# Matmul with rotary embedding: tiles worked in pairs over three PSUM banks, one multiply per pair, and one tile in four transposed by VectorE

## The chip, the cores and the metric

One core of a Trainium2 chip. The time is the device time of one execution in microseconds. The kernel before ran at 168.18 us, the median of three runs (166.9 to 168.86). A "beat" below is the time TensorE takes for one tile, or one pair of tiles, in the steady part of the kernel. All verdicts and ratios use runs of the state called fast; the medians are over all runs, and those of e1, e5 and e10 include runs of the slow state.

## The reference

```python
# x (16, 512, 768), weight (768, 768), cos and sin (512, 64), 12 heads of 64 columns, all fp32
y = np.matmul(x, weight).reshape(batch, seq, n_heads, head_dim)
y1, y2 = y[..., :32], y[..., 32:]
out1 = y1 * cos1 - y2 * sin1
out2 = y2 * cos2 + y1 * sin2
out = np.concatenate([out1, out2], axis=-1).reshape(batch, seq, hidden)
```

There are 16 x 512 = 8192 rows, which is 64 tiles of 128 rows. For every tile the contraction runs over the 768 columns of x, and the kernel before turns every tile (columns onto partitions) for the matmuls: 384 transposes on TensorE, six a tile, in its profile.

## The kernel before

Every tile is loaded by the SyncE ring (a ring is the queue of transfers that one engine's sequencer issues), cast to fp16 by ScalarE, turned by six TensorE transposes into PSUM (the memory that TensorE writes its results to), copied back by ScalarE, multiplied with the weights by twelve matmuls, and then combined by two VectorE multiplies and one GpSimd (POOL) add. The ScalarE ring stores.

```python
def load(i):
    xss[i] = xpool.tile([P, H], FP32, tag="xs", name="xs")
    nc.sync.dma_start(out=xss[i], in_=xv[i // SB, i % SB])
...
def transpose(i, eng):
    xc = x16.pop(i)
    pt = pt_pool.tile([P, NKT, P], FP16, tag="pt", name="pt")
    for kt in range(NKT):
        nc.tensor.transpose(pt[:, kt, :], xc[:, ts(kt, P)], ident)
    xTT[i] = tpool.tile([P, NKT, P], FP16, tag="xT", name="xT")
    copy(eng, xTT[i], pt)
...
for i in range(FIRST, NMB):
    if i + AHEAD - FIRST < NMB:
        load(i + AHEAD - FIRST)
    if i + 1 < NMB:
        transpose(i + 1, nc.scalar)
    if 4 < i + 2 < NMB:
        cast(i + 2, nc.scalar)
    if i < NMB - 1:
        for kt in range(NKT):
            mm(i, kt)
        rope_whole(i)
        store(i - 3)
```

Of the kernel before, what the change touches and what calls it, by code (L numbers as in the profile page):

```python
# [10 lines left out]
FP32 = mybir.dt.float32  # L11
# [6 lines left out]
def kernel(  # L18
# [16 lines left out]
    NKT = H // P  # L35
    NMB = B * S // P
    SB = S // P
    NSPLIT = [(0, 512), (512, H - 512)]
    HALVES = [(0, H // 2), (H // 2, H // 2)]
    FIRST = 3  # L40
    AHEAD = 8


    xv = x.rearrange("b (p r) h -> b r p h", r=SB)
    ov_dram = out.rearrange("b (p r) h -> b r p h", r=SB)
# [3 lines left out]
    cos_sb = konst.tile([P, SB, D], FP32)  # L49
    tee_sb = konst.tile([P, SB, D], FP32)  # L50
    w_raw = konst.tile([P, NKT, H], FP32)
    w_sb = konst.tile([P, NKT, H], FP16)

    xpool = ctx.enter_context(tc.tile_pool(name="xpool", bufs=AHEAD + 3))
    cpool = ctx.enter_context(tc.tile_pool(name="cpool", bufs=4))
    tpool = ctx.enter_context(tc.tile_pool(name="tpool", bufs=FIRST + 2))
    rpool = ctx.enter_context(tc.tile_pool(name="rpool", bufs=4))
    opool = ctx.enter_context(tc.tile_pool(name="opool", bufs=5))
    pt_pool = ctx.enter_context(tc.tile_pool(name="pt", bufs=2, space=bass.MemoryType.PSUM))
    py_pool = ctx.enter_context(tc.tile_pool(name="py", bufs=3, space=bass.MemoryType.PSUM))  # L60

    cold = konst.tile([P, 512], FP16)
    cold_ps = pt_pool.tile([P, 512], FP32, tag="pt", name="cold_ps")

    xss, x16, xTT, psys, ovs = {}, {}, {}, {}, {}
# [7 lines left out]
    def load(i):  # L73
        xss[i] = xpool.tile([P, H], FP32, tag="xs", name="xs")
        nc.sync.dma_start(out=xss[i], in_=xv[i // SB, i % SB])  # L75

    wv = weight.rearrange("(kt p) n -> p kt n", p=P)

    def load_w(kt):
        nc.sync.dma_start(out=w_raw[:, kt], in_=wv[:, kt])  # L80

    def cast_w(kt):
        nc.vector.tensor_copy(out=w_sb[:, kt], in_=w_raw[:, kt])  # L83

    def cast(i, eng):
        x16[i] = cpool.tile([P, H], FP16, tag="xc", name="xc")
        copy(eng, x16[i], xss.pop(i))

    def transpose(i, eng):
        xc = x16.pop(i)  # L90
        pt = pt_pool.tile([P, NKT, P], FP16, tag="pt", name="pt")
        for kt in range(NKT):
            nc.tensor.transpose(pt[:, kt, :], xc[:, ts(kt, P)], ident)  # L93
        xTT[i] = tpool.tile([P, NKT, P], FP16, tag="xT", name="xT")
        copy(eng, xTT[i], pt)

    def mm(i, kt, parts=NSPLIT):
        if i not in psys:
            psys[i] = py_pool.tile([P, 2, 512], FP32, tag="psy", name="psy").rearrange(
                "p b n -> p (b n)"  # L100
            )
        for noff, nsz in parts:
            nc.tensor.matmul(  # L103
                psys[i][:, ds(noff, nsz)],
                xTT[i][:, kt, :],
                w_sb[:, kt, ds(noff % H, nsz)],
                start=(kt == 0),
                stop=(kt == NKT - 1),
            )

    def rope(i, c0, n, ps, add_eng):
        sb = i % SB
        nh = n // D
        tv = rpool.tile([P, H], FP32, tag="tv", name="tv")[:, :n]
        qv = rpool.tile([P, H], FP32, tag="qv", name="qv")[:, :n]
        nc.vector.tensor_tensor(  # L116
            out=tv.rearrange("p (h d) -> p h d", d=D),
            in0=ps.rearrange("p (h d) -> p h d", d=D),
            in1=cos_sb[:, sb, :].unsqueeze(1).broadcast_to((P, nh, D)),
            op=MULT,  # L120
        )
        nc.vector.tensor_tensor(  # L122
            out=qv.rearrange("p (h t d) -> p h t d", t=2, d=HD),
            in0=ps.rearrange("p (h t d) -> p h t d", t=2, d=HD)[:, :, ::-1, :],
            in1=tee_sb[:, sb, :].rearrange("p (t d) -> p t d", t=2)
            .unsqueeze(1).broadcast_to((P, nh, 2, HD)),
            op=MULT,
        )
        ov = ovs[i]
        add_eng.tensor_tensor(out=ov[:, ds(c0, n)], in0=tv, in1=qv, op=ADD)  # L130

    def rope_whole(i):
        ovs[i] = opool.tile([P, H], FP32, tag="ov", name="ov")
        rope(i, 0, H, psys.pop(i)[:, 0:H], nc.gpsimd)

    def store(i):
        nc.scalar.dma_start(out=ov_dram[i // SB, i % SB], in_=ovs.pop(i))

    def warm(n):
        for _ in range(n):  # L140
            nc.tensor.matmul(cold_ps, cold[:, 0:P], cold, start=True, stop=True)  # L141
# [6 lines left out]
    load(0)  # L148
    load_w(0)
    load_w(1)  # L150
    load(1)
    nc.scalar.dma_start(out=cos_sb, in_=cos.rearrange("(p r) d -> p r d", r=SB))
    nc.scalar.dma_start(out=tee_sb, in_=sin.rearrange("(p r) d -> p r d", r=SB))
    load_w(2)
    load_w(3)
    load(2)
    load_w(4)
    load_w(5)
    for i in range(FIRST, AHEAD):
        load(i)  # L160

    warm(9)
    cast(0, nc.vector)
    transpose(0, nc.vector)
    warm(4)
    for kt in (0, 1):
        cast_w(kt)
        mm(0, kt)
# [10 lines left out]
    for kt in range(4):  # L179
        mm(2, kt)  # L180
# [82 lines left out]
```

## Time and profile before

| | kernel before |
|---|---|
| span of the profiled run | 166.9 us |
| PE (TensorE matmul) busy | 153.6 us, 92% |
| POOL, DVE (VectorE), ACT (ScalarE) busy | 114.4, 122.9, 97.9 us |
| beat of one tile | 2.285 us |
| regular beat begins | 20.9 us |
| last matmul ends, and what follows | 160.1 us, then 6.8 us |

These are lines of part 2 of the page: the span cut into 40 slices of 4.2 us, each digit the busy share of one slice in tenths.

```profile
PE   7657699999999999999999999999999999999930
...
ACT  3053366667766667766667766667666667666400
...
DMA  4999999999999999999999999999999984345544
```

PE is at 9 from the sixth slice to the last but two; ACT is at 6 or 7. The DMA row also shows 9, but it does so in opening slices that moved 403 GB/s as well as in later ones that moved 330, so a 9 there does not say that no more could be moved. Part 4 of the page is the chain of work that ended last, as shares of the span, by engine and then by line:

```profile
PE 88%; DMA 4%; ACT 2%; DVE 2%; issue 1%; SPq 1%; DVEq 0%
PE psy L103 74%; PE pt L93 13%; DMA xs<-in_x_dram 4%; PE psy L216 1%; DVE ov L130 1%; ACT xc L69 1%; ACT xT L69 1%; DVE qv L122 1%; SPq L80 1%; DVE tv L116 0%; SPq L75 0%; DVEq L130 0%; DVEq L116 0%
```

74% of the chain are the matmuls (psy), 13% the PE transposes (pt). The costliest groups of part 5 (line, engine, operation, output and inputs, count | busy us, mean ns of one | idle us of the engine before them and what ended it):

```profile
L130 POOL TENSOR_TENSOR ov<-tv,qv 128x768 f32<-128x768 f32 x63 | 114.2, 1816 | 47.4 <-DVE qv L122 46.2
L103 PE MATMUL psy<-w_sb,xT 128*128 128x512 f16 x756 | 135.1, 329 | 2.5 <-ACT xT L69 1.8
...
L116 DVE TENSOR_TENSOR tv<-psy,cos_sb 128x768 f32<-128x768 f32 (+1 forms) x65 | 61.4, 944 | 31.7 <-PE psy L103 30.5
...
L69 ACT CAST xc<-xs 128x768 f16<-128x768 f32 x63 | 52.7, 836 | 5.8 <-DMA xs<-in_x_dram 5.8
L93 PE MATMUL pt<-ident,xc 128*128 128x128 f16 x384 | 31.9, 219 | 2.9 <-ACT xc L69 2.2
```

The last figures say who waits for whom: POOL and DVE wait, PE does not (2.5 us in all over 756 matmuls). The matmul durations overlap (756 of 329 ns would be 249 us, and their busy time is 135.1), so they are no beat. The beat is read from the timeline (start us, length us, engine, what), here the PE lines of two successive tiles:

```profile
23.19 0.50 PE L93 MATMUL pt<-ident,xc 128*128 128x128 f16 x6
...
25.47 0.50 PE L93 MATMUL pt<-ident,xc 128*128 128x128 f16 x6
```

The six transposes come at 23.19 and again at 25.47; over many tiles the beat is 2.285 us, of which the chain gives 1.95 to the twelve matmuls and 0.335 to the transposes. The last matmuls of the kernel are here:

```profile
158.00 2.11 PE L216 MATMUL psy<-w_sb,xT 128*128 128x384 f16 x12
```

They end at 158.00 + 2.11 = 160.11 us. The other 6.8 us of the span are the tail.

### The profile page before, as it was taken

What the parts mean: (1) busy time and instruction counts of PE and PEld (TensorE: products, weight loads), DVE (VectorE), ACT (ScalarE), POOL (GpSimd) and SP (SyncE); (2) the same over time, 40 slices, a digit from 0 to 9 for tenths busy, and PEclk for the clock granted to TensorE, in tenths of its full rate; (3) what the DMA queues carried; (4) which work ended last, traced back from release to release, by engine and by line L of the source; (5) the groups of instructions that cost most, each with busy time, mean ns of one, the idle gap of its engine ahead of it and who ended that gap; (6) DMA issues with size and microseconds to landing.
All of it is one profiled execution on the core that took longest, in us unless ns stands there. A gap on an engine that the chain in (4) does not pass through costs nothing.

```text
span 166.9 us, 3136 instructions
## 1 busy us (share of the span) xinstructions
PE 153.6 (92%) x1165; PEld 98.5 (59%) x1165; DVE 122.9 (74%) x142; ACT 97.9 (59%) x127; POOL 114.4 (69%) x67
## 2 busy tenths in 40 slices
PE   7657699999999999999999999999999999999930
PEld 2224466666666666666666666666666666666610
DVE  0522598777877688877778877778877778777792
ACT  3053366667766667766667766667666667666400
POOL 0000099777787777887777887777887777877770
PEclk9987999999999999999999999999999999999997
DMA  4999999999999999999999999999999984345544
GB/s 128 405 402 403 403 404 369 301 375 406 340 372 343 328 350 345 350 326 381 335 327 370 347 330 351 337 327 361 368 349 350 300 323 170 146 161 192 213 166 188
DMA packets 19887, 53.19 MB, mean 319 GB/s; under 512 B 2336, under 2 KB 2848, under 8 KB 19872
## 3 DMA queue, kind: packets, MB, share of 16 engines
q1 hardware_dynamic: 10368, 27.92, 49.5%
q10 hardware_dynamic: 9504, 25.07, 37.8%
q8 instruction: 9, 0.15, 0.5%
q14 instruction: 6, 0.05, 0.1%
HBM read 27.82 MB, written 25.17 MB: 317 GB/s over the span
## 4 chain that ended last, share of the span: by engine, by line
PE 88%; DMA 4%; ACT 2%; DVE 2%; issue 1%; SPq 1%; DVEq 0%
PE psy L103 74%; PE pt L93 13%; DMA xs<-in_x_dram 4%; PE psy L216 1%; DVE ov L130 1%; ACT xc L69 1%; ACT xT L69 1%; DVE qv L122 1%; SPq L80 1%; DVE tv L116 0%; SPq L75 0%; DVEq L130 0%; DVEq L116 0%
## 5 line engine op out<-in xcount | busy, mean ns | idle before, releaser
L130 POOL TENSOR_TENSOR ov<-tv,qv 128x768 f32<-128x768 f32 x63 | 114.2, 1816 | 47.4 <-DVE qv L122 46.2
L103 PE MATMUL psy<-w_sb,xT 128*128 128x512 f16 x756 | 135.1, 329 | 2.5 <-ACT xT L69 1.8
L103 PEld LDWEIGHTS <-xT 128*128 128x128 f16 x756 | 71.8, 99 | 44.9 <-ACT xT L69 2.1
L116 DVE TENSOR_TENSOR tv<-psy,cos_sb 128x768 f32<-128x768 f32 (+1 forms) x65 | 61.4, 944 | 31.7 <-PE psy L103 30.5
L69 ACT COPY xT<-pt 128x768 f16<-128x768 f16 x63 | 50.3, 798 | 51.2 <-PE pt L93 51.2
L122 DVE TENSOR_TENSOR qv<-psy,tee_sb 128x768 f32<-128x768 f32 (+1 forms) x65 | 60.7, 934 | 0.0
L69 ACT CAST xc<-xs 128x768 f16<-128x768 f32 x63 | 52.7, 836 | 5.8 <-DMA xs<-in_x_dram 5.8
L93 PE MATMUL pt<-ident,xc 128*128 128x128 f16 x384 | 31.9, 219 | 2.9 <-ACT xc L69 2.2
L93 PEld LDWEIGHTS <-xc 128*128 128x128 f16 x384 | 26.6, 98 | 12.3 <-ACT xc L69 3.0
L83 DVE CAST w_sb<-w_raw 128x768 f16<-128x768 f32 x6 | 3.3, 558 | 4.1 <-DMA w_raw<-in_weight_dram 4.1
L141 PE MATMUL cold_ps<-cold 128*128 128x512 f16 x13 | 4.6, 514 | 1.2 <-DVE cold L146 1.2
L141 PEld LDWEIGHTS <-cold 128*128 128x128 f16 x13 | 1.5, 126 | 3.3 <-issue 1.9
L71 DVE CAST xc<-xs 128x768 f16<-128x768 f32 x1 | 0.6, 560 | 3.7 <-DMA xs<-in_x_dram 3.7
L69 ACT ACT_TABLE_LOAD x1 | 1.3, 1283 | 2.1 <-issue 2.1
L216 PE MATMUL psy<-w_sb,xT 128*128 128x384 f16 x12 | 2.1, 326 | 0.0
L130 DVE TENSOR_TENSOR ov<-tv,qv 128x384 f32<-128x384 f32 x2 | 1.7, 862 | 0.1
L216 PEld LDWEIGHTS <-xT 128*128 128x128 f16 x12 | 1.2, 98 | 0.8
L71 DVE COPY xT<-pt 128x768 f16<-128x768 f16 x1 | 0.6, 556 | 0.6 <-PE pt L93 0.6
L146 DVE MEMSET cold<- 128x256 uint32 x1 | 0.3, 272 | 0.9 <-PEq L244 0.9
L244 POOL MEMSET const-float32-0.0<- 128x1 f32 x1 | 0.1, 98 | 0.2 <-issue 0.2
L185 DVE TENSOR_SCALAR tee_sb<-tee_sb 128x128 f32<-128x128 f32 x1 | 0.2, 220 | 0.0
L244 POOL MEMSET const-bfloat16-1.0<- 128x1 bf16 x1 | 0.1, 101 | 0.0
(2 smaller groups left out, 0.2 us busy)
## 6 DMA issues: line engine op xcount, KB each, us to landing
xs<-in_x_dram SPq DMA_DIRECT2D x64, 384.0 KB, 5.6
out_dram<-ov ACTq DMA_DIRECT2D x63, 384.0 KB, 4.8
w_raw<-in_weight_dram SPq DMA_DIRECT2D x6, 384.0 KB, 5.9
out_dram<-ov SPq DMA_DIRECT2D x2, 192.0 KB, 2.2
cos_sb<-in_cos_dram ACTq DMA_DIRECT2D x1, 128.0 KB, 5.2
tee_sb<-in_sin_dram ACTq DMA_DIRECT2D x1, 128.0 KB, 6.2
ident<-identity ACTq DMA_DIRECT2D x1, 32.0 KB, 3.6
```

The lines of the kernel that those rows point to most:

```text
L69: eng.copy(out=o, in_=i_)
L71: eng.tensor_copy(out=o, in_=i_)
L80: nc.sync.dma_start(out=w_raw[:, kt], in_=wv[:, kt])
L83: nc.vector.tensor_copy(out=w_sb[:, kt], in_=w_raw[:, kt])
L93: nc.tensor.transpose(pt[:, kt, :], xc[:, ts(kt, P)], ident)
L103: nc.tensor.matmul(psys[i][:, ds(noff, nsz)], xTT[i][:, kt, :], w_sb[:, kt, ds(noff % H, nsz)], start=(kt == 0), stop=(kt == NKT - 1),)
L116: nc.vector.tensor_tensor(out=tv.rearrange("p (h d) -> p h d", d=D), in0=ps.rearrange("p (h d) -> p h d", d=D), in1=cos_sb[:, sb, :].unsqu ...
L122: nc.vector.tensor_tensor(out=qv.rearrange("p (h t d) -> p h t d", t=2, d=HD), in0=ps.rearrange("p (h t d) -> p h t d", t=2, d=HD)[:, :, : ...
L130: add_eng.tensor_tensor(out=ov[:, ds(c0, n)], in0=tv, in1=qv, op=ADD)
L141: nc.tensor.matmul(cold_ps, cold[:, 0:P], cold, start=True, stop=True)
L146: nc.vector.memset(cold, 0.0)
L216: nc.tensor.matmul(psys[i][:, n, 0:sz], xTT[i][:, kt, :], w_sb[:, kt, ds(c0, sz)], start=(kt == 0), stop=(kt == NKT - 1),)
```

## The change

Its intent was to take work off TensorE. In every second pair, one of the two tiles is not sent through TensorE but turned by VectorE in blocks of 32 x 32. For that the program brings the tile in with a different part of the columns on each group of 32 partitions: it is loaded by four transfers of 32 partitions each, two from the SyncE ring and two from the ScalarE ring. VectorE pays for this work by doing one multiply over a pair (3072 results) instead of four. The pair's sums take three PSUM banks (a tile of 3 x 512 fp32 in the program), and there are two such buffers. Contraction columns are taken in a new order, so that a pair of fp16 values is turned as one fp32 (128x384 f32, for 768 fp16); for this the casts read x with a stride. The change also runs 26 warm-up matmuls on zeros instead of 13, and loads cos and sin from the SyncE ring. The core of the diff:

```diff
+    def by_blocks(n, s):
+        return n > 2 and n % 2 == 1 and s == 1
...
+    DEPTH = 8
+    xpool = ctx.enter_context(tc.tile_pool(name="xpool", bufs=2 * DEPTH + 2))
-    py_pool = ctx.enter_context(tc.tile_pool(name="py", bufs=3, space=bass.MemoryType.PSUM))
+    py_pool = ctx.enter_context(tc.tile_pool(name="py", bufs=2, space=bass.MemoryType.PSUM))
...
+    def load(n, s):
+        b, r = where(n, s)
+        xs = xpool.tile([P, H], FP32, tag="xs", name="xs")
+        if by_blocks(n, s):
+            xs = xs.rearrange("p (j k) -> p j k", j=NQ)
+            src = x[b].rearrange("(j a r) (q k) -> r q a j k", r=SB, a=R, q=NQ)
+            for q in (0, 2, 1, 3):
+                eng = nc.sync if q < 2 else nc.scalar
+                eng.dma_start(out=xs[ts(q, R)], in_=src[r, q])
+        else:
+            nc.sync.dma_start(
+                out=xs, in_=x[b].rearrange("(p r) h -> r p h", r=SB)[r]
+            )
...
+    def cast(n, s, eng):
+        if by_blocks(n, s):
+            src = src.rearrange("p j (a t e) -> p t (j a) e", t=NT, e=2)
+        else:
+            src = src.rearrange("p (m i) -> p i m", m=P)     # every sixth fp32
+        copy(eng, xc, src)
...
+    def transpose_blocks(n, s):
+        xT = tpool.tile([P, NT, P, 2], FP16, tag="xT", name="xT")
+        nc.vector.transpose(
+            out=xT.bitcast(FP32).rearrange("p t m e -> p (t m e)"),
+            in_=x16.pop((n, s)).bitcast(FP32),
+        )
...
         nc.vector.tensor_tensor(
-            out=tv..., in0=ps..., in1=cos_sb..., op=MULT)
-        nc.vector.tensor_tensor(
-            out=qv..., in0=ps... halves swapped, in1=tee_sb..., op=MULT)
+            out=tq.rearrange("p j (h d) -> p j h d", d=D),
+            in0=psys[n]... read twice, in1=csn[:, :, r, :]..., op=MULT)
...
+    # before the main loop, in this order
+    for n in (0, 1):
+        for s in (0, 1):
+            load(n, s)
+    for t, e in CHUNKS:
+        load_w(t, e)
+    load(2, 0)
+    ... cos, sin ...
+    load(2, 1)
+    for n in range(3, DEPTH):
+        for s in (0, 1):
+            load(n, s)
...
+    cast(0, 0, nc.vector)
+    transpose(0, 0, nc.vector)
+    cast(0, 1, nc.scalar)          # ScalarE's first work
```

There are 32 pairs, and 15 of the 64 tiles go by blocks.

More of the change, by code (lines that the diff above doesn't have):

```diff
@@ L34, with where @@
     HD = D // 2
-    NKT = H // P
-    NMB = B * S // P
+    R = 32
+    NQ = P // R
+    NT = H // (2 * P)
     SB = S // P
-    NSPLIT = [(0, 512), (512, H - 512)]
-    HALVES = [(0, H // 2), (H // 2, H // 2)]
-    FIRST = 3
-    AHEAD = 8
-    xv = x.rearrange("b (p r) h -> b r p h", r=SB)
-    ov_dram = out.rearrange("b (p r) h -> b r p h", r=SB)
+    NP = B * SB // 2
+    CHUNKS = [(t, e) for t in range(NT) for e in range(2)]
+    DEPTH = 8
+    TAIL = 2
+    def where(n, s):
+        return 2 * (n // SB) + s, n % SB
+    def by_blocks(n, s):
+        return n > 2 and n % 2 == 1 and s == 1
     konst = ctx.enter_context(tc.tile_pool(name="konst", bufs=1))
     ident = konst.tile([P, P], FP16)
-    cos_sb = konst.tile([P, SB, D], FP32)
-    tee_sb = konst.tile([P, SB, D], FP32)
-    w_raw = konst.tile([P, NKT, H], FP32)
-    w_sb = konst.tile([P, NKT, H], FP16)
-    xpool = ctx.enter_context(tc.tile_pool(name="xpool", bufs=AHEAD + 3))
-    cpool = ctx.enter_context(tc.tile_pool(name="cpool", bufs=4))
-    tpool = ctx.enter_context(tc.tile_pool(name="tpool", bufs=FIRST + 2))
-    rpool = ctx.enter_context(tc.tile_pool(name="rpool", bufs=4))
-    opool = ctx.enter_context(tc.tile_pool(name="opool", bufs=5))
+    cold = konst.tile([P, 512], FP16)
+    sin_sb = konst.tile([P, SB, D], FP32)
+    csn = konst.tile([P, 2, SB, D], FP32)
+    w_raw = konst.tile([P, NT, 2, H], FP32)
+    w_sb = konst.tile([P, NT, 2, H], FP16)
+    xpool = ctx.enter_context(tc.tile_pool(name="xpool", bufs=2 * DEPTH + 2))
+    cpool = ctx.enter_context(tc.tile_pool(name="cpool", bufs=6))
+    tpool = ctx.enter_context(tc.tile_pool(name="tpool", bufs=7))
+    rpool = ctx.enter_context(tc.tile_pool(name="rpool", bufs=3))
+    opool = ctx.enter_context(tc.tile_pool(name="opool", bufs=4))
     pt_pool = ctx.enter_context(tc.tile_pool(name="pt", bufs=2, space=bass.MemoryType.PSUM))
-    py_pool = ctx.enter_context(tc.tile_pool(name="py", bufs=3, space=bass.MemoryType.PSUM))
-    cold = konst.tile([P, 512], FP16)
+    py_pool = ctx.enter_context(tc.tile_pool(name="py", bufs=2, space=bass.MemoryType.PSUM))
     cold_ps = pt_pool.tile([P, 512], FP32, tag="pt", name="cold_ps")
-    xss, x16, xTT, psys, ovs = {}, {}, {}, {}, {}
+    xss, x16, xTT, psys, tqs, ovs = {}, {}, {}, {}, {}, {}
     def copy(eng, o, i_):
@@ L71, in copy @@
             eng.tensor_copy(out=o, in_=i_)
-    def load(i):
-        xss[i] = xpool.tile([P, H], FP32, tag="xs", name="xs")
-        nc.sync.dma_start(out=xss[i], in_=xv[i // SB, i % SB])
-    wv = weight.rearrange("(kt p) n -> p kt n", p=P)
-    def load_w(kt):
-        nc.sync.dma_start(out=w_raw[:, kt], in_=wv[:, kt])
-    def cast_w(kt):
-        nc.vector.tensor_copy(out=w_sb[:, kt], in_=w_raw[:, kt])
-    def cast(i, eng):
-        x16[i] = cpool.tile([P, H], FP16, tag="xc", name="xc")
-        copy(eng, x16[i], xss.pop(i))
@@ L89, in transpose @@
-    def transpose(i, eng):
-        xc = x16.pop(i)
-        pt = pt_pool.tile([P, NKT, P], FP16, tag="pt", name="pt")
-        for kt in range(NKT):
-            nc.tensor.transpose(pt[:, kt, :], xc[:, ts(kt, P)], ident)
-        xTT[i] = tpool.tile([P, NKT, P], FP16, tag="xT", name="xT")
-        copy(eng, xTT[i], pt)
-    def mm(i, kt, parts=NSPLIT):
-        if i not in psys:
-            psys[i] = py_pool.tile([P, 2, 512], FP32, tag="psy", name="psy").rearrange(
+    def load(n, s):
[11 more added lines that the diff above has]
+            )
+        xss[n, s] = xs
@@ new lines, with load_w, cast_w @@
+    wv = weight.rearrange("(p t e) n -> t e p n", t=NT, e=2)
+    def load_w(t, e):
+        nc.sync.dma_start(out=w_raw[:, t, e], in_=wv[t, e])
+    def cast_w(t, e):
+        nc.vector.tensor_copy(out=w_sb[:, t, e], in_=w_raw[:, t, e])
+    def cast(n, s, eng):
+        xc = cpool.tile([P, H], FP16, tag="xc", name="xc")
+        src = xss.pop((n, s))
+        if by_blocks(n, s):
+            x16[n, s] = xc
+            xc = xc.rearrange("p (t m e) -> p t m e", t=NT, e=2)
+            src = src.rearrange("p j (a t e) -> p t (j a) e", t=NT, e=2)
+        else:
+            xc = xc.rearrange("p (i m) -> p i m", m=P)
+            x16[n, s] = xc
+            src = src.rearrange("p (m i) -> p i m", m=P)
+        copy(eng, xc, src)
@@ new lines, in transpose @@
+    def transpose(n, s, eng):
+        xc = x16.pop((n, s))
+        pt = pt_pool.tile([P, NT, 2, P], FP16, tag="pt", name="pt")
+        for t, e in CHUNKS:
+            nc.tensor.transpose(pt[:, t, e, :], xc[:, 2 * t + e, :], ident)
+        xT = tpool.tile([P, NT, 2, P], FP16, tag="xT", name="xT")
+        copy(eng, xT, pt)
+        xTT[n, s] = xT
+    def transpose_blocks(n, s):
[4 more added lines that the diff above has]
+        )
+        xTT[n, s] = xT.rearrange("p t m e -> p t e m")
@@ L100, in mm @@
+    def mm(n, s, t, e, c0=0, c1=H):
+        if n not in psys:
+            psys[n] = py_pool.tile([P, 3, 512], FP32, tag="psy", name="psy").rearrange(
                 "p b n -> p (b n)"
             )
-        for noff, nsz in parts:
-            nc.tensor.matmul(
-                psys[i][:, ds(noff, nsz)],
-                xTT[i][:, kt, :],
-                w_sb[:, kt, ds(noff % H, nsz)],
-                start=(kt == 0),
-                stop=(kt == NKT - 1),
-            )
-    def rope(i, c0, n, ps, add_eng):
-        sb = i % SB
-        nh = n // D
-        tv = rpool.tile([P, H], FP32, tag="tv", name="tv")[:, :n]
-        qv = rpool.tile([P, H], FP32, tag="qv", name="qv")[:, :n]
+            if n < 2:
+                nc.tensor.matmul(
+                    psys[n][:, 512:1024], cold[:, 0:P], cold, start=True, stop=False
+                )
+        cut = 512 if s == 0 else 256
+        for lo, hi in ((0, cut), (cut, H)):
+            lo, hi = max(lo, c0), min(hi, c1)
+            joined = n < 2 and 512 <= s * H + lo < 1024
+            if lo < hi:
+                nc.tensor.matmul(
+                    psys[n][:, ds(s * H + lo, hi - lo)],
+                    xTT[n, s][:, t, e, :],
+                    w_sb[:, t, e, ds(lo, hi - lo)],
+                    start=((t, e) == CHUNKS[0] and not joined),
+                    stop=((t, e) == CHUNKS[-1] and not (joined and s == 0)),
+                )
@@ L116, in rope @@
+    def rope(n, c0, c1, add_eng):
+        r = n % SB
+        w = c1 - c0
+        nh = w // D
+        if n not in tqs:
+            tqs[n] = rpool.tile([P, 2, 2 * H], FP32, tag="tq", name="tq")
+            ovs[n] = opool.tile([P, 2 * H], FP32, tag="ov", name="ov")
+        tq = tqs[n][:, :, ds(c0, w)]
+        ov = ovs[n][:, ds(c0, w)]
         nc.vector.tensor_tensor(
-            out=tv.rearrange("p (h d) -> p h d", d=D),
-            in0=ps.rearrange("p (h d) -> p h d", d=D),
-            in1=cos_sb[:, sb, :].unsqueeze(1).broadcast_to((P, nh, D)),
+            out=tq.rearrange("p j (h d) -> p j h d", d=D),
+            in0=psys[n][:, ds(c0, w)].rearrange("p (h d) -> p h d", d=D)
+            .unsqueeze(1).broadcast_to((P, 2, nh, D)),
+            in1=csn[:, :, r, :].unsqueeze(2).broadcast_to((P, 2, nh, D)),
@@ L120, in rope @@
             op=MULT,
         )
-        nc.vector.tensor_tensor(
-            out=qv.rearrange("p (h t d) -> p h t d", t=2, d=HD),
-            in0=ps.rearrange("p (h t d) -> p h t d", t=2, d=HD)[:, :, ::-1, :],
-            in1=tee_sb[:, sb, :].rearrange("p (t d) -> p t d", t=2)
-            .unsqueeze(1).broadcast_to((P, nh, 2, HD)),
-            op=MULT,
-        )
-        ov = ovs[i]
-        add_eng.tensor_tensor(out=ov[:, ds(c0, n)], in0=tv, in1=qv, op=ADD)
-    def rope_whole(i):
-        ovs[i] = opool.tile([P, H], FP32, tag="ov", name="ov")
-        rope(i, 0, H, psys.pop(i)[:, 0:H], nc.gpsimd)
@@ L136, in store @@
-    def store(i):
-        nc.scalar.dma_start(out=ov_dram[i // SB, i % SB], in_=ovs.pop(i))
-    def warm(n):
-        for _ in range(n):
+        add_eng.tensor_tensor(
+            out=ov.rearrange("p (h t d) -> p h t d", t=2, d=HD),
+            in0=tq[:, 0].rearrange("p (h t d) -> p h t d", t=2, d=HD),
+            in1=tq[:, 1].rearrange("p (h t d) -> p h t d", t=2, d=HD)[:, :, ::-1, :],
+            op=ADD,
+        )
+    def store(n, eng, c0=0, c1=2 * H):
+        b, r = where(n, 0)
+        dst = out.rearrange("b (p r) h -> r p b h", r=SB)[r, :, b : b + 2]
+        src = ovs[n].rearrange("p (b h) -> p b h", b=2)
+        if c1 - c0 < 2 * H:
+            s = c0 // H
+            dst = dst[:, s, c0 - s * H : c1 - s * H]
+            src = src[:, s, c0 - s * H : c1 - s * H]
+        eng.dma_start(out=dst, in_=src)
@@ L141, in warm @@
+    def warm(k):
+        for _ in range(k):
             nc.tensor.matmul(cold_ps, cold[:, 0:P], cold, start=True, stop=True)
@@ L147 @@
     nc.scalar.dma_start(out=ident, in_=id_dram.ap())
-    load(0)
-    load_w(0)
-    load_w(1)
-    load(1)
-    nc.scalar.dma_start(out=cos_sb, in_=cos.rearrange("(p r) d -> p r d", r=SB))
-    nc.scalar.dma_start(out=tee_sb, in_=sin.rearrange("(p r) d -> p r d", r=SB))
-    load_w(2)
-    load_w(3)
-    load(2)
-    load_w(4)
-    load_w(5)
-    for i in range(FIRST, AHEAD):
-        load(i)
-    warm(9)
-    cast(0, nc.vector)
-    transpose(0, nc.vector)
-    warm(4)
-    for kt in (0, 1):
-        cast_w(kt)
-        mm(0, kt)
@@ L169 @@
-    cast(1, nc.scalar)
-    transpose(1, nc.scalar)
-    mm(1, 0)
-    mm(1, 1)
-    for kt in (2, 3):
-        cast_w(kt)
-        mm(0, kt)
-        mm(1, kt)
-    cast(2, nc.scalar)
-    transpose(2, nc.scalar)
-    for kt in range(4):
-        mm(2, kt)
-    cast_w(4)
-    for i in range(FIRST):
-        mm(i, 4)
-    cast_w(5)
+    for n in (0, 1):
+        for s in (0, 1):
+            load(n, s)
+    for t, e in CHUNKS:
+        load_w(t, e)
+    load(2, 0)
+    nc.sync.dma_start(out=csn[:, 0], in_=cos.rearrange("(p r) d -> p r d", r=SB))
@@ new lines, with prepare_a, prepare_b @@
+    nc.sync.dma_start(out=sin_sb, in_=sin.rearrange("(p r) d -> p r d", r=SB))
+    load(2, 1)
+    for n in range(3, DEPTH):
+        for s in (0, 1):
+            load(n, s)
+    def prepare_a(n, s):
+        if n < NP:
+            cast(n, s, nc.scalar)
+    def prepare_b(n, s):
+        if n < NP and not by_blocks(n, s):
+            transpose(n, s, nc.scalar)
+    warm(10)
+    cast(0, 0, nc.vector)
+    transpose(0, 0, nc.vector)
+    cast(0, 1, nc.scalar)
+    warm(4)
+    transpose(0, 1, nc.scalar)
@@ L185 @@
+    cast(1, 0, nc.vector)
+    warm(4)
+    transpose(1, 0, nc.vector)
+    cast(1, 1, nc.scalar)
+    warm(4)
+    transpose(1, 1, nc.scalar)
+    warm(4)
+    for k, c in enumerate(CHUNKS):
+        cast_w(*c)
+        mm(0, 0, *c)
+        mm(0, 1, *c)
+        if k > 0:
+            mm(1, 0, *CHUNKS[k - 1])
+    nc.vector.tensor_copy(out=csn[:, 1, :, 0:HD], in_=sin_sb[:, :, HD:D])
     nc.vector.tensor_scalar_mul(
-        out=tee_sb[:, :, 0:HD], in0=tee_sb[:, :, 0:HD], scalar1=-1.0
+        out=csn[:, 1, :, HD:D], in0=sin_sb[:, :, 0:HD], scalar1=-1.0
@@ L187 @@
     )
-    cast(3, nc.scalar)
-    mm(0, 5)
-    rope_whole(0)
-    mm(1, 5)
-    rope_whole(1)
-    transpose(3, nc.scalar)
-    cast(4, nc.scalar)
-    mm(2, 5)
-    rope_whole(2)
-    for i in range(FIRST, NMB):
-        if i + AHEAD - FIRST < NMB:
-            load(i + AHEAD - FIRST)
-        if i + 1 < NMB:
-            transpose(i + 1, nc.scalar)
-        if 4 < i + 2 < NMB:
-            cast(i + 2, nc.scalar)
-        if i < NMB - 1:
-            for kt in range(NKT):
-                mm(i, kt)
-            rope_whole(i)
-            store(i - 3)
@@ L210 @@
-    i = NMB - 1
-    ovs[i] = opool.tile([P, H], FP32, tag="ov", name="ov")
-    for n, (c0, sz) in enumerate(HALVES):
-        for kt in range(NKT):
-            if i not in psys:
-                psys[i] = py_pool.tile([P, 2, 512], FP32, tag="psy", name="psy")
-            nc.tensor.matmul(
-                psys[i][:, n, 0:sz],
-                xTT[i][:, kt, :],
-                w_sb[:, kt, ds(c0, sz)],
-                start=(kt == 0),
-                stop=(kt == NKT - 1),
-            )
-    for j in range(NMB - 4, NMB - 1):
-        store(j)
@@ L225 @@
-    for n, (c0, sz) in enumerate(HALVES):
-        rope(i, c0, sz, psys[i][:, n, 0:sz], nc.vector)
-        nc.sync.dma_start(out=ov_dram[i // SB, i % SB, :, ds(c0, sz)], in_=ovs[i][:, ds(c0, sz)])
+    rope(0, 0, 2 * H, nc.gpsimd)
+    prepare_a(2, 0)
+    prepare_a(2, 1)
+    mm(1, 0, *CHUNKS[-1])
+    for c in CHUNKS:
+        mm(1, 1, *c)
+    prepare_b(2, 0)
+    prepare_a(3, 0)
+    prepare_b(2, 1)
+    prepare_a(3, 1)
+    rope(1, 0, 2 * H, nc.gpsimd)
+    for n in range(2, NP):
+        if n + DEPTH - 2 < NP:
+            for s in (0, 1):
+                load(n + DEPTH - 2, s)
+        if n + 1 < NP and by_blocks(n + 1, 1):
+            transpose_blocks(n + 1, 1)
+        if n < NP - 1:
+            for c in CHUNKS:
+                mm(n, 0, *c)
+            prepare_b(n + 1, 0)
+            prepare_a(n + 2, 0)
+            for c in CHUNKS:
+                mm(n, 1, *c)
+            prepare_b(n + 1, 1)
+            prepare_a(n + 2, 1)
+            if n >= 3:
+                store(n - 3, nc.scalar)
+            if n < NP - 2:
+                rope(n, 0, 2 * H, nc.gpsimd)
+            else:
+                rope(n, 0, H, nc.gpsimd)
+                rope(n, H, 2 * H, nc.gpsimd)
@@ new lines @@
+    n = NP - 1
+    for c in CHUNKS:
+        mm(n, 0, *c)
+    cut = H // 3
+    for c in CHUNKS:
+        mm(n, 1, *c, cut, H)
+    for c in CHUNKS:
+        mm(n, 1, *c, 0, cut)
+    store(n - 3, nc.scalar)
+    store(n - 2, nc.scalar)
+    rope(n, 0, H // 2, nc.gpsimd)
+    rope(n, H // 2, H, nc.gpsimd)
+    store(n - 1, nc.sync)
+    store(n, nc.scalar, 0, H)
+    rope(n, H + cut, 2 * H, nc.gpsimd)
+    rope(n, H, H + cut, nc.vector)
+    store(n, nc.sync, H, H + cut)
+    store(n, nc.scalar, H + cut, 2 * H)
```

## The prediction

> **What bounds the kernel now.** TensorE. The chain of waits puts 88% of the 166.9 us span on PE: 74% on the matmuls, 13% on the PE transposes. In the timeline every tile from 21 to 160 us takes 2.285 us: 1.95 us of matmuls (12 of them) and 0.335 us of transposes (six). In the table by stretches PE is busy throughout at clock 1.00; of 23 us DVE is busy 18.4, ACT 15.4, POOL 18.3. Around that lie a start (the beat begins at 20.9 us, three tiles' matmuls done) and a tail (last matmul 160.1, end 166.9: 6.8 us).
>
> **What the change removes.** 15 of 64 tiles lose their PE transposes: 15 x 0.335 = 5.0 us of PE, all on the chain. ACT loses their 798 ns copies.
>
> **What it adds or moves, per pair of tiles.** The new PE beat is 4.57 us (even pairs) or 4.24 us (odd), mean 4.40.
> - DVE: four 950 ns multiplies become one over 3072 elements. From 957 ns for 768 and 550 ns for 384 elements the slope is 1.06 ns per element plus 0.14, so about 3.4 us (estimate). The block transpose of 384 fp32 adds about 0.55 us in odd pairs (same slope[...]). At most 3.95 of 4.24: fits. But only two PSUM buffers remain: a pair's multiply must end before the pair after next begins; slack 0.8 to 1.2 us.
> - POOL: 1536-element add, about 3.6 us (twice 1816 ns). Fits if the half-swapped read costs nothing.
> - ACT: two casts (836 ns) now reading every sixth fp32, one or two 798 ns copies, 0.34 us per DMA issue: 3.6 us at most, if stride is free.
> - Stationary loads with 4-byte steps: 98 ns now[...].
> - DMA: 15 tiles as 768-byte pieces in 32-partition transfers. [...] prefetch is 16 tiles deep. Not limiting, but close.
>
> **Start.** The last weight piece is the tenth load instead of the ninth (1 us each), but pair 1 is transposed meanwhile. PSUM frees for pair 2 when the first 3.4 us multiply ends, about 19.5 us, with four tiles' matmuls and six tiles' transposes done. Remaining PE: 60 x 1.95 + 43 x 0.335 = 131.4 us, so the last matmul ends near 151, against 160.1. About 4 us of this gain is the start, 5 the transposes.
>
> **Tail.** Coarser steps leave POOL further behind: I estimate 8.5 us instead of 6.8.
>
> **Prediction.** 151 + 8.5, plus 1 us by which the median time exceeds the profiled one: 160.5 us, range 156.5 to 166.5. Chances: faster 0.75, same 0.15, slower 0.10.
>
> **What would show it.** PE still 85% or more of the chain; PE transposes 294 instead of 384; steady pairs averaging 4.4 us in the timeline; pair multiply 3.3 to 3.5 us; cast still about 840 ns; pair add about 3.6 us; the beat starting near 19.5; an 8 to 9 us tail.
>
> **What would make it wrong.** Strided casts slow (above 1.4 us ACT becomes the bound); the swapped add over 4.4 us (POOL becomes the bound); [...]block loads so slow that ACT waits for data or its DMA issues stall; PE waiting for PSUM each pair.

## The result, and the profile after

The changed kernel took 184.95 us, the median of four runs (184.3 to 185.15), against 167.66 us for the kernel before in the same rounds. The ratio is 1.102 (95% interval 1.094 to 1.110): slower by 10%. Ratios here and below are the mean time of one kernel's fast runs over that of the other's of the same rounds, so they are not quite the ratio of the medians. The profiled span was 183.4 us. The same lines of the page's part 2, now slices of 4.6 us, with the granted TensorE clock:

```profile
PE   7400008998999999999999999999999999999910
...
ACT  0000046707989898989898989898989888898000
...
PEclk9975555999999999999999999999999999999995
DMA  5999999930869999999999999999993836353967
```

Slices 3 to 6 have no PE work at all, ACT does nothing in the first five, and the clock falls to 5 tenths. From slice 11 on PE is at 9 as before. DMA falls to 0 in slice 10: the load buffers are full, and SyncE waits for casts to free them (7.1 us at the longest, by its own list of waits). So the loss lies in the first 45 us. The chain by engine and line:

```profile
PE 75%; DMA 11%; POOL 3%; issue 2%; ACT 2%; DVE 2%; SPq 2%; POOLq 1%; ACTq 0%; DVEq 0%
PE psy L147 64%; PE pt L118 9%; DMA xs<-in_x_dram 7%; DMA w_raw<-in_weight_dram 4%; POOL ov L171 3%; PE cold_ps L190 2%; DVE tq L164 2%; SPq L88 1%; ACT xc L74 1%; POOLq L324 1%; SPq L96 1%; ACT L74 1%; ACT xT L74 0%; PE psy L139 0%; ACTq L86 0%
```

The groups that answer to those of before:

```profile
L171 POOL TENSOR_TENSOR ov<-tq 128x1536 f32<-128x1536 f32 (+3 forms) x35 | 110.8, 3172 | 69.1 <-DVE tq L164 69.1
L147 PE MATMUL psy<-w_sb,xT 128*128 128x512 f16 (+1 forms) x768 | 132.3, 326 | 0.6 <-ACT xT L74 0.6
L164 DVE TENSOR_TENSOR tq<-psy,csn 128x3072 f32<-128x3072 f32 (+4 forms) x36 | 107.6, 3000 | 28.5 <-PE psy L147 28.5
...
L74 ACT CAST xc<-xs 128x768 f16<-128x768 f32 x62 | 87.5, 1437 | 0.0
...
L118 PE MATMUL pt<-ident,xc 128*128 128x128 f16 x294 | 24.9, 223 | 21.5 <-ACT xc L74 21.5
...
L125 DVE STREAM_TRANSPOSE xT<-xc 128x384 f32<-128x384 f32 x15 | 8.5, 569 | 0.2 <-ACT xc L74 0.2
```

The steady part did what was planned: 90 fewer PE transposes, one multiply a pair, a POOL add for two tiles, and 569 ns for a block transpose. Only one item is not as predicted: the casts, at 1437 ns instead of 836. (That is a mean: 47 casts of tiles for TensorE at about 1.6 us and 15 of block tiles at about 0.9.) PE idles 21.5 us before its transposes, all of it in one wait for a ScalarE cast (xc): that is the loss as this view shows it. The end is as planned. The last matmuls:

```profile
168.91 6.01 PE L147 MATMUL psy<-w_sb,xT 128*128 128x256 f16 x36
```

They end at 174.92 us, and 8.5 us follow. Now the beginning. Here is the chain of waits in order of time (start us, length us, what), its longest pieces only:

```profile
4.01 8.12 DMA w_raw<-in_weight_dram
...
12.16 6.95 DMA xs<-in_x_dram
...
19.12 5.72 DMA xs<-in_x_dram
...
25.21 1.28 ACT L74
...
26.51 1.55 ACT xc L74
...
43.35 2.12 PE psy L147 x12
```

and ScalarE's own timeline, with ACTq for the transfers that its sequencer issues:

```profile
12.16 13.03 ACTq L86 DMA_DIRECT2D xs<-in_x_dram  x6
25.21 1.28 ACT L74 ACT_TABLE_LOAD   x1 [25.21 <-DMA xs<-in_x_dram]
26.51 1.54 ACT L74 CAST xc<-xs 128x768 f16<-128x768 f32 x1
```

ScalarE casts nothing before 26.5 us. Until 25.2 us its sequencer is occupied with six transfer issues, which are the halves of the block tiles of pairs 3, 5 and 7. In the chain, the end of each waiting piece is the start of the next: a weight load issued at 4.01 lands at 12.13, a load issued at 12.16 lands at 19.11, one issued at 19.12 lands at 24.84, and then ScalarE runs. The matmuls of pair 2 (the first regular beat) begin at 43.35 us, where the prediction had 19.5.

The times of issue and landing of all transfers in this trace show what the issues wait for. Of the 152 transfers of both rings, never more than eight were in flight at once (nor of the 138 in the trace of the kernel before). Counted in order of issue, each of the transfers 11 to 36 was issued 0.02 us after the landing of the transfer eight places before it (one, the 22nd, 0.11 us), whichever ring that was on. This is every eighth of them:

```
place  issued by  what                      issued   landed   eight places before, landed
  1    ScalarE    identity                   0.73     3.77    -
  9    SyncE      weight piece 4 of 6        4.01    12.13     3.77
 17    ScalarE    pair 3, block q=2         12.16    19.11    12.13
 25    SyncE      pair 5, block q=0         19.12    24.84    19.11
 33    ScalarE    pair 7, block q=3         24.87    30.76    24.84
```

That is link for link the chain above: 4.01, 12.16, 19.12, then, when the last of these has landed at 24.84, the sixth ScalarE issue. (The ninth began when SyncE's issue before it had ended, at 3.97.) The six ScalarE issues began at 12.16, 14.14, 18.89, 19.39, 24.09 and 24.87 us, and the transfers eight places before them landed at 12.13, 14.12, 18.86, 19.37, 24.07 and 24.84. How the wait is built was not measured.

### The profile page after: what moved, and what is told of

Read it like the earlier page. It is cut to its first block, busy times and chain, and to the rows that moved or that the text cites. A ratio compares the mean times of both kernels' runs of the same rounds, so it can differ in the third digit from the quotient of the medians.

```text
span 183.4 us, 2763 instructions
## 1 busy us (share of the span) xinstructions
PE 151.7 (83%) x1090; PEld 95.5 (52%) x1090; DVE 121.6 (66%) x65; ACT 121.2 (66%) x110; POOL 111.0 (61%) x39
## 4 chain that ended last, share of the span: by engine, by line
PE 75%; DMA 11%; POOL 3%; issue 2%; ACT 2%; DVE 2%; SPq 2%; POOLq 1%; ACTq 0%; DVEq 0%
PE psy L147 64%; PE pt L118 9%; DMA xs<-in_x_dram 7%; DMA w_raw<-in_weight_dram 4%; POOL ov L171 3%; PE cold_ps L190 2%; DVE tq L164 2%; SPq L88 1%; ACT xc L74 1%; POOLq L324 1%; SPq L96 1%; ACT L74 1%; ACT xT L74 0%; PE psy L139 0%; ACTq L86 0%
## 5 line engine op out<-in xcount | busy, mean ns | idle before, releaser
L171 POOL TENSOR_TENSOR ov<-tq 128x1536 f32<-128x1536 f32 (+3 forms) x35 | 110.8, 3172 | 69.1 <-DVE tq L164 69.1
L147 PE MATMUL psy<-w_sb,xT 128*128 128x512 f16 (+1 forms) x768 | 132.3, 326 | 0.6 <-ACT xT L74 0.6
L164 DVE TENSOR_TENSOR tq<-psy,csn 128x3072 f32<-128x3072 f32 (+4 forms) x36 | 107.6, 3000 | 28.5 <-PE psy L147 28.5
L74 ACT CAST xc<-xs 128x768 f16<-128x768 f32 x62 | 87.5, 1437 | 0.0
L74 ACT COPY xT<-pt 128x768 f16<-128x768 f16 x47 | 37.6, 799 | 23.6 <-PE pt L118 23.5
L118 PE MATMUL pt<-ident,xc 128*128 128x128 f16 x294 | 24.9, 223 | 21.5 <-ACT xc L74 21.5
L118 PEld LDWEIGHTS <-xc 128*128 128x128 f16 x294 | 20.9, 100 | 29.0 <-ACT xc L74 22.0
L74 ACT ACT_TABLE_LOAD x1 | 1.3, 1283 | 25.2 <-DMA xs<-in_x_dram 25.2
L190 PE MATMUL cold_ps<-cold 128*128 128x512 f16 x26 | 9.8, 530 | 1.2 <-DVE cold L195 1.2
L125 DVE STREAM_TRANSPOSE xT<-xc 128x384 f32<-128x384 f32 x15 | 8.5, 569 | 0.2 <-ACT xc L74 0.2
L190 PEld LDWEIGHTS <-cold 128*128 128x128 f16 x26 | 3.2, 131 | 5.0 <-issue 3.3
L139 PEld LDWEIGHTS <-cold 128*128 128x128 f16 x2 | 0.2, 98 | 0.1
```

The lines of the kernel that those rows point to most:

```text
L74: eng.copy(out=o, in_=i_)
L118: nc.tensor.transpose(pt[:, t, e, :], xc[:, 2 * t + e, :], ident)
L125: nc.vector.transpose(out=xT.bitcast(FP32).rearrange("p t m e -> p (t m e)"), in_=x16.pop((n, s)).bitcast(FP32),)
L147: nc.tensor.matmul(psys[n][:, ds(s * H + lo, hi - lo)], xTT[n, s][:, t, e, :], w_sb[:, t, e, ds(lo, hi - lo)], start=((t, e) == CHUNKS[0] ...
L164: nc.vector.tensor_tensor(out=tq.rearrange("p j (h d) -> p j h d", d=D), in0=psys[n][:, ds(c0, w)].rearrange("p (h d) -> p h d", d=D) .uns ...
L171: add_eng.tensor_tensor(out=ov.rearrange("p (h t d) -> p h t d", t=2, d=HD), in0=tq[:, 0].rearrange("p (h t d) -> p h t d", t=2, d=HD), in ...
```

## The experiments

Theory A: six of ScalarE's transfer issues stand in front of its first cast (in the trace they lie between 12.16 and 25.18 us, the cast at 26.51), and each waits for an earlier transfer, so the start is lost there. Theory B: the 32-partition transfers are slow in themselves and hold up everything. Theory C: the strided casts and the wide multiply cost the time. Twelve kernels ran, each in rounds with the kernel before on the same chip.

| run | what differs from the changed kernel | median us | ratio to before (95%) | pair 2 begins |
|---|---|---|---|---|
| (changed) | | 184.95 | 1.102 (1.094 to 1.110) | 43.35 |
| e1 | block loads before the loop on SyncE | 172.87 | 1.022 (1.012 to 1.031) | 21.13 |
| e2 | no blocks, but 128-partition loads on ScalarE | 184.23 | 1.101 (1.094 to 1.108) | 37.52 |
| e4 | all loads on SyncE | 162.60 | 0.973 (0.966 to 0.980) | 20.64 |
| e5 | four pairs ahead instead of eight | 189.29 | 1.129 (1.121 to 1.137) | 32.34 |
| e3 | no blocks, all loads on SyncE | 167.79 | 1.003 (0.997 to 1.009) | 20.64 |
| e12 | e3 with plain column order | 167.01 | 0.998 (0.993 to 1.003) | 19.82 |
| e7 | e4, block tile in one transfer (wrong result) | 162.89 | 0.974 (0.969 to 0.979) | 21.20 |
| e8 | e4, blocks in every pair | 173.77 | 1.039 (1.033 to 1.044) | 20.87 |
| e10 | e8 with whole rows (wrong result) | 173.52 | 1.027 (1.018 to 1.035) | 21.24 |
| e11 | e8 over all partitions (wrong result) | 177.50 | 1.057 (1.050 to 1.065) | 20.74 |
| e9 | blocks merged over two batches | 165.31 | 0.991 (0.985 to 0.997) | 21.08 |
| e14 | e4, blocks in two pairs of three | 162.06 | 0.969 (0.964 to 0.974) | 20.76 |

### e4: all loads on the SyncE ring

```diff
-                eng = nc.sync if q < 2 else nc.scalar
+                eng = nc.sync
```

> All 32-partition transfers on the SyncE ring, none on ScalarE. Theory A: beat at 19.5 to 20.5 us, time 161 to 162 us, like e1. Theory B: slower than e1[...]: casts wait for data in the loop and the time is over 165 us.

Measured: 162.6 us (theory A: 161 to 162), and 2.7% faster than the kernel before. The outputs are right. The chain of waits of e4:

```profile
1.17 4.11 DMA xs<-in_x_dram
...
5.30 1.59 ACT xc L74
...
20.64 2.12 PE psy L147 x12
```

ScalarE's first cast begins when its tile has landed, at 5.3 us, and pair 2 begins at 20.64 us. The profiled span is 160.7 us, which is 22.7 less than the changed kernel's 183.4; the start of pair 2 moved by 43.35 - 20.64 = 22.7. So the whole loss lies in the start, and one changed line removes it. Of the 22.7 us, 21.2 are the later first cast (26.51 against 5.30 us). The other 1.5 lie between that cast and pair 2; there the granted clock averaged 0.82 in the changed kernel (26 to 43 us); over the whole span it was 0.93 in the changed kernel and 0.98 in e4. In the steady part of e4 PE waits for nothing: over the whole run its matmuls on psy waited once, 0.6 us, at the start of pair 2.

### e1: only the loads before the loop moved

```diff
-                eng = nc.sync if q < 2 else nc.scalar
+                eng = nc.sync if q < 2 or n < DEPTH else nc.scalar
```

> Only the six block-load issues that stand before the main loop move from the ScalarE ring to the SyncE ring; in the loop they stay on ScalarE. Theory A (the ScalarE sequencer stands still behind those six issues until 25.2 us, because each waits for the eighth-last transfer of the whole program): the first ScalarE cast moves from 26.5 us to about 6, the beat (first matmuls of pair 2) from 43.35 to 19.5 to 20.5, the time to about 161 to 162 us. Theory B (32-partition transfers are slow and hold everything up by themselves): the same transfers still go out, so the beat stays near 40 us and the time at 180 or more. Theory C (slow strided casts and the single wide multiply cost the time): no change, 185.

Measured: 172.9 us, the median of two slow runs (174.2 and 174.3) and two fast ones (170.5 and 171.5). The fast runs miss theory A's 161 to 162 us by 9 to 10 us, so theory A as stated was incomplete; the numbers of B (180 or more) and C (185) are missed too. The first cast did come early (5.5 us), and pair 2 began at 21.13. But the first passes of the loop also issue block loads from ScalarE, and there they wait again. From the chain of waits of e1 (its profile is of a run in the slow state; it is used for the waits alone):

```profile
18.27 6.61 DMA xs<-in_x_dram
...
24.90 6.10 DMA xs<-in_x_dram
...
36.23 7.00 DMA xs<-in_x_dram
...
49.16 6.84 DMA xs<-in_x_dram
...
57.26 3.07 PE psy L147 x12
```

These are the last four waits on transfers of the chain, 6 to 7 us each, and the last is over at 56 us. PE paused three times in this stretch, 7.5 us in all. After 65 us e1 runs at the regular beat. So the same wait comes twice: before the loop, and again in its first passes. e4 removes both.

### e2: the ScalarE ring without 32-partition transfers

```diff
-        return n > 2 and n % 2 == 1 and s == 1
+        return False
...
-            nc.sync.dma_start(
+            eng = nc.scalar if n > 2 and n % 2 == 1 and s == 1 else nc.sync
+            eng.dma_start(
```

> No tile by blocks: every load is one 128-partition transfer and every tile goes through the PE transposes, but the second tile of each odd pair is still loaded from the ScalarE ring, three of them before the loop. Theory A: ScalarE still stands, though shorter: the last of its three issues waits for the transfer eight places earlier, the 17th, which I put at about 17 us, so the beat begins near 35 us. With 15 more tiles of PE transposes (5 us) and all casts strided (about 1.56 us each, which brings ScalarE to 4.6 us a pair) the time is 181 to 186 us. Theory B: without 32-partition transfers the start is that of the kernel before, beat near 20 us, about 167 us.

Measured: 184.2 us, with pair 2 at 37.5 us. This is theory A's number; theory B's was 167. There is no 32-partition transfer in this kernel, and the start is lost all the same: ScalarE is held until 19.0 us by three ordinary loads. e3 below is the same kernel with these loads on SyncE: pair 2 at 20.64 and 167.8 us.

### e5: a shorter queue before the loop

```diff
-    DEPTH = 8
+    DEPTH = 4
```

> Loads run four pairs ahead instead of eight, so only pair 3's block tile is issued before the loop: two ScalarE issues instead of six. Theory A: the last of these waits for the last weight transfer, seen at 14.1 us in the changed kernel, so ScalarE starts near 14.5 instead of 25.2, the beat near 32.5, the time 173 to 175 us. Theory B: the start is little changed, as the first tiles and weights come in the same order; 183 or more.

Measured: the start was as theory A said, the total was not. The chain of waits of e5:

```profile
5.26 8.44 DMA w_raw<-in_weight_dram
...
14.07 1.28 ACT L74
...
32.34 2.12 PE psy L147 x12
...
45.22 9.46 DMA xs<-in_x_dram
...
57.24 7.93 DMA xs<-in_x_dram
```

ScalarE was free at 14.07 us (expected: 14.5) and pair 2 began at 32.34 (expected: 32.5). But then the loop, with only four pairs of lead, had a wait of 7 to 9.5 us on a transfer about every 10 us, and the total was 189.3 us, not 173 to 175; it lies where theory B's total was put (183 or more), though B's start does not fit. How much of that comes from ScalarE's issues in the loop and how much from the short lead was not separated. For the start, this run is the closest test of theory A: two issues instead of six, and the delay shrinks to the landing of the transfer that the second one waits for.

### e3 and e12: what the blocks are worth, and what the stride costs

```diff
 # e3: by_blocks returns False, so every load is on SyncE and every tile goes through PE
-        return n > 2 and n % 2 == 1 and s == 1
+        return False
 # e12: e3, and in addition
-            src = src.rearrange("p (m i) -> p i m", m=P)
+            src = src.rearrange("p (i m) -> p i m", m=P)
-    wv = weight.rearrange("(p t e) n -> t e p n", t=NT, e=2)
+    wv = weight.rearrange("(t e p) n -> t e p n", t=NT, e=2)
```

> Pairs with one multiply as in the changed kernel, but no tile by blocks and every load on the SyncE ring. If the block transposes are worth their PE time once the start is clean: 15 x 0.335 = 5.0 us more than e4, so about 167.5 us, the same as the kernel before within 1%. The beat should be 4.57 us a pair, with ScalarE full (two casts of 1.58 and two copies of 0.70 net, seen in e2). If the block path brings nothing, it equals e4's 162.6.

> e3 with columns and weight rows in their plain order, so that the casts read contiguous fp32. Casts fall from about 1.58 to 0.84 us and ScalarE from 100% to about 70% of the steady part. If TensorE bounds e3, the time stays within 1% of e3; if the slow casts bound it (theory C), it is over 2% faster.

e3 took 167.8 us: with the ring question out of the way, the block transposes are worth 5.2 us (e3 against e4, medians). In the profiles the last matmul ends at 157.24 in e3 and at 152.21 in e4, which is 5.03 us for 15 x 0.335. Pairs alone are worth nothing (1.003). The casts of e3, then of e12, in the groups by shape:

```profile
L74 ACT CAST xc<-xs 128x768 f16<-128x768 f32 x62 | 100.2, 1616 | 6.3 <-DMA xs<-in_x_dram 6.2
```

```profile
L74 ACT CAST xc<-xs 128x768 f16<-128x768 f32 x62 | 51.8, 836 | 9.2 <-DMA xs<-in_x_dram 9.2
```

The stride nearly doubles the cast: 1616 ns with a step of 24 bytes (e3), 836 in order (e12), and 913, close to that, for the block tiles, which read two neighbours at a time (the ScalarE casts from the merged block tiles in e9). VectorE's cast went from 560 ns in the kernel before to 838 in the changed one with the same step. Why was not measured. The busy time of each engine between 60 and 100 us, first e3, then e12 (columns: stretch, its length, then PE, PEld, DVE, ACT, POOL busy with counts, granted clock, DMA share, GB/s):

```profile
60.00:100.00 40.00, 40.00 (x315) 26.30 (x314) 29.09 (x10) 39.96 (x36) 33.77 (x10) 1.00 0.99 376
```

```profile
60.00:100.00 40.00, 40.00 (x319) 26.54 (x318) 29.40 (x9) 26.43 (x35) 33.05 (x10) 1.00 1.00 377
```

In e3 ScalarE is busy 39.96 of 40 us, and yet PE is busy throughout too: both just fit. Theory C is out as the cause of the loss, since e12 is within 1% of e3, and e3 with slow casts and wide multiply is no slower than the kernel before. But e3 shows that the slow casts leave ScalarE no slack unless some tiles go by blocks.

### e7: the 32-partition transfers taken away

```diff
-            for q in (0, 2, 1, 3):
-                eng = nc.sync if q < 2 else nc.scalar
-                eng.dma_start(out=xs[ts(q, R)], in_=src[r, q])
+            nc.sync.dma_start(
+                out=xs,
+                in_=x[b].rearrange("(p r) (j k) -> r p j k", r=SB, j=NQ)[r],
+            )
```

> Wrong results on purpose: e4 with each block tile loaded by one 128-partition transfer of 3072-byte rows (the bytes land in the wrong partitions), all else the same. It takes the 32-partition transfers away. If they cost time only through the place they take among the eight transfers in flight, off the critical path on the SyncE ring: within 1% of e4, 161.5 to 163 us. Theory B: over 2% faster than e4.

Measured: 162.9 us, the same as e4. Where 15 tiles go by blocks and nothing of it is on ScalarE, the small transfers cost no time. Theory B is out.

### e8, e10, e11: how far it goes

```diff
 # e8: e4, and
-        return n > 2 and n % 2 == 1 and s == 1
+        return n > 2 and s == 1
 # e10: e8, each transfer 32 partitions but whole rows of 3072 bytes (wrong result)
-                eng.dma_start(out=xs[ts(q, R)], in_=src[r, q])
+                nc.sync.dma_start(out=xs[ts(q, R)], in_=rows[r, ts(q, R)])
 # e11: e8, each transfer all 128 partitions, 768 bytes each (wrong result)
+                nc.sync.dma_start(out=xs[:, q], in_=cols[r, :, q])
```

> e4 with one tile by blocks in every pair from pair 3 on (29 tiles instead of 15), all on SyncE. TensorE alone would save 14 x 0.335 = 4.7 us more: 158 us. But each pair then needs six transfers (one plain, four small, one store) and at most eight are in flight, each landing about 6.3 us after issue, so one pair takes about 6 / 8 x 6.3 = 4.7 us against TensorE's 4.24: if that limit holds, casts wait for data and the time is 165 to 172 us.

> Wrong results on purpose: e8 with its four 32-partition transfers a tile kept, 96 KB each, but reading whole rows of 3072 bytes instead of pieces of 768. If the number of transfers is the limit, as slow as e8: 170 to 175 us. If the short pieces are, near the 158 us that TensorE allows.

> Wrong results on purpose: e8 with its four transfers a tile of 96 KB each and its pieces of 768 bytes, but each transfer now spans all 128 partitions and a quarter of the columns instead of 32 partitions. If the number of transfers (six a pair, eight in flight) is e8's limit, it stays at 170 to 175 us. If the reach of 32 partitions is, it falls towards the 158 us that TensorE allows.

With a block tile in every pair the gain turns into a loss: 173.8 us, a little over the range I had given. The largest waits of e8 on transfers, and PE's:

```profile
ACT xc L74 <- DMA xs<-in_x_dram: 45.4, 31, 3.6
POOL ov L171 <- DMA out_dram<-ov: 31.1, 11, 4.7
...
PE psy L147 <- ACT xT L74: 13.7, 14, 2.2
```

Casts wait 45 us for tiles. e10 has longer pieces (3072 bytes), e11 reaches all partitions; neither comes near the 158 us that TensorE allows (173.5 and 177.5; by the ratios e10 may be 1% better than e8, e11 is worse). What the three share is the size and number of the transfers: four of 96 KB a tile, six transfers a pair. So neither the short pieces alone nor the reach alone is what limits e8. No run removed both at six transfers a pair. e9, below, has the same pieces and reach for 26 tiles, but fewer transfers, and took 165.3 us, which points to the number of transfers.

The estimate from eight in flight (the most in the traces before and after; six of eight, 6.3 us each, makes 4.7 us a pair) seems to fit: the pairs of e8 took 4.76 us on average, (163.55 - 20.87) / 30. But it used the landing time of e4, and in e8 loads landed sooner, by part 6 of its page (the last number is the median us from issue to landing):

```profile
xs<-in_x_dram SPq DMA_DIRECT2D x35, 384.0 KB, 5.0
xs<-in_x_dram SPq DMA_DIRECT2D x116, 96.0 KB, 4.6
```

With 5.9 us for a store (the same part of the page), six transfers make (4 x 4.6 + 5.0 + 5.9) / 8 = 3.7 us a pair (estimate), less than TensorE's 4.24, if eight were always in flight. By the same numbers it was 29.3 / 4.76 = 6.2 on average (estimate), and that 4.7 came out close is luck. In e10, which issues as many transfers of the same sizes, SyncE's own list of waits puts 44.7 us, in 17 waits before 32-partition loads (L86), down to stores that had not landed. So the cause of e8's loss is narrowed down, not shown; it was not tested by allowing more than eight in flight. In e11 part of the waiting was of another kind (ScalarE's copies waited 21.3 us for stores to land), so its waits are not those of e8 one for one.

### e9 and e14: two attempts at a better version

```diff
 # e9: tiles of a pair eight batches apart; block tiles of two batches share transfers of 192 KB
-        return 2 * (n // SB) + s, n % SB
+        return n // SB + s * (B // 2), n % SB
-        return n > 2 and n % 2 == 1 and s == 1
+        return s == 1 and (n >= 8 or n in (5, 7))
...
+            src = x[b : b + 1 + both].rearrange(
+                "b (j a r) (q k) -> r q a (b j) k", r=SB, a=R, q=NQ)
 # e14: e4, and
-        return n > 2 and n % 2 == 1 and s == 1
+        return n > 2 and n % 3 != 2 and s == 1
```

> A version meant to beat all others. The two tiles of a pair come from batches eight apart, so that block tiles of neighbouring batches can share their four 32-partition transfers: 192 KB each, still pieces of 768 bytes. 26 tiles go by blocks (24 in shared transfers, 2 alone), all on SyncE. If e8 was slow because of the number of transfers (six a pair, eight in flight), here it is four a pair on average and TensorE bounds again: matmuls from 20.6 us, plus 60 x 1.95 + 32 x 0.335 = 127.7, plus a tail of 8.4, so 156.7 profiled and about 158 us in time. If the 768-byte pieces or the 32-partition reach themselves were the limit, it stays near e8's 174 or at best at e4's 163.

> A version meant to beat e4: block tiles in two pairs of three from pair 3 on (20 tiles instead of 15, I count n = 3, 4, 6, 7 and so on to 31), all on SyncE. Transfers rise to about 5.0 a pair; at e4's landing time of 6.3 us and eight in flight that takes 3.9 us, still under TensorE's mean of about 4.35 us a pair, but with little to spare. If it holds: 5 x 0.335 = 1.7 us less than e4, so about 159.0 profiled and 161 in time. If the transfers bind, 163 to 168.

e9 failed: 165.3 us instead of 158, between that and e8, so neither side of its expectation was met. It has fewer transfers, but four pairs in a row load five each, and there PE had to wait for tiles (4.9 us in four waits, 0.6 of it at the start as in e4), with loads and stores in turn in the chain (a store from 117.53 to 125.63 us, a load from 125.65 to 131.11, a store from 131.20). That the bursts are the cause is argued from the chain, not tested. e14 took 162.06 us. Its matmuls end at 150.66 us against e4's 152.21, the 1.6 us that five more block tiles should bring (1.7 expected), but its tail is 0.3 us longer, and in time its interval (0.964 to 0.974) overlaps e4's. It beats the kernel before by 3%; that it beats e4 is not shown.

## Why the prediction was wrong, point by point

- **What bounds the kernel: right.** PE is without gaps in the steady part before and after, and the pairs of the changed kernel take the 4.4 us that was predicted, on average: pair 2 to the last matmul is 174.92 - 43.35 = 131.6 us for 30 pairs; the prediction had 131.4.
- **The 5.0 us of PE transposes: right.** 5.03 us between e3 and e4.
- **VectorE, POOL, stationary loads: right.** Multiply 3357 ns (3.4 us predicted), block transpose 569 ns (0.55), pair add 3467 ns (3.6), stationary loads 98 ns as before.
- **Tail: right.** 8.5 us, as predicted.
- **ScalarE's casts: wrong, but not on the path.** "If stride is free": it is not, 1616 ns. The prediction's bound of 1.4 us for ScalarE was also not right, as e3 with 1616 ns still kept up with TensorE, just.
- **Start: this is the step that failed.** The prediction said "PSUM frees for pair 2 when the first 3.4 us multiply ends, about 19.5 us". It was 43.35 us. The prediction costed ScalarE's share in the loads as "0.34 us per DMA issue", the duration of an issue without its wait (338 ns, the median of its 63 store issues in the kernel before). In the changed kernel six such issues stood in front of ScalarE's first cast, and each waited for an older transfer to land; they held ScalarE to 25.2 us. With the same loads on SyncE (e4) pair 2 begins at 20.64, 1.1 us from the prediction, and the time is 162.6 us, inside the predicted range. Even there the last wait was not the one predicted: the first multiply ended at about 20.2 us, and PE then waited for ScalarE's copy of pair 2's first tile, which ended at 20.59.
- **DMA "not limiting, but close": right for 15 block tiles on SyncE (e7 is the same as e4), but by the wrong measure.** I had counted bytes, with an assumption about 32-partition transfers that no run shows. What held the start was the wait of an issue for an older transfer (ScalarE's until 25.2 us), which such a count does not show. e8, with more and smaller transfers, lost time as well, though its cause is only narrowed down.
- The list of what would make it wrong did name "its DMA issues stall". But the start was computed as if that could not happen, although the trace of before held the sign: SyncE's issues of weight loads (L80) waited for the identity, cosine and sine transfers of the other ring. These are lines of the SyncE queue's own list of waits in the kernel before (who, on what: us in total, times, longest):

```profile
SPq L80 <- DMA tee_sb<-in_sin_dram: 1.2, 1, 1.2
SPq L80 <- DMA cos_sb<-in_cos_dram: 1.2, 1, 1.2
SPq L80 <- DMA ident<-identity: 1.1, 1, 1.1
```

A ring that waits for the other ring's transfers was there to be read before predicting.

## What to carry to other kernels

A transfer issued from ScalarE's queue was here a wait in ScalarE's own program (its first cast at 26.51 us, against 5.30 with those loads on SyncE). Before issuing from a compute engine, ask what the issue may wait for (here the transfer eight places before, on either ring), and do not put prefetches of later tiles in front of the engine's first work. When large transfers are cut into small ones, count the transfers and ask what each issue waits for, not the bytes alone (e8, with six transfers a pair, took 173.8 us and e4 162.6). When a well-costed change comes out slower, look for slices in which the busiest engine does nothing before doubting the costs: all 22.7 us lost here lay before the steady part.
